# Where two gate-vector chunks of layer 0 are multiplied, and which memory the feed-forward weight buffers lie over

## The chip, the cores and the metric

The kernel runs on one core of a Trainium2 chip. The metric is the device time of one execution in microseconds (us). In the profile the engines are PE (TensorE), ACT (ScalarE), DVE (VectorE), POOL (GpSimd) and SP (SyncE, which here issues most of the DMA transfers); PEld is PE's loading of stationary operands.

## The reference, cut to what matters

Two layers work on 256 context tokens and 256 latent tokens of width 1024. The parts around the change:

```
mod = silu(c) @ mod_w[layer] + mod_b[layer]      # 6 vectors of 1024, for c and for c_ctx
sh1, sc1, g1, sh2, sc2, g2 = split(mod, 6)
x = x + g1 * even_mixer(rmsnorm(x, g) * (1 + sc1) + sh1)
x = x + g2 * conv_ffn(rmsnorm(x, g) * (1 + sc2) + sh2)
# layer 1: the same with odd_mixer, then a final rmsnorm
```

The mixer of layer 0 has two head groups (GLA and mLSTM), whose outputs are normalised, joined and multiplied by an output projection of 1024 x 1024. The feed-forward is an up projection to 2 x 2816 columns, a depthwise convolution, silu(g) * a, and a down projection.

## The kernel before, in words

Activations lie transposed, features on partitions and the 512 tokens along the free axis, so each 128 x 128 block of a weight is multiplied with 512 columns. For float32 accuracy each weight block and each activation is split into a high and a low half (wh, wl; hh, hl), and three matmuls (L186 to L188) make one product.

**Weights** come through `Stream` (L144): one load brings 16 blocks, 1 MB, into a raw tile; `split` turns 8 blocks, a unit, into wh by a copy on ACT (L174) and wl by a subtraction on DVE or POOL (L175), in the pool `wp` with 4 slots for each. `get` (L178) splits one unit ahead of the one in use. With a list `fill`, each load of a stream from number `skip` on also calls one function of the list (L161, L162), so that other work is spread over the stream.

**The modulation vectors** are such work. A chunk (layer, j) is 512 columns of `mod_w`: `mod_load` (L236) loads 2 MB in n pieces on SP, `mod_go` (L244) multiplies them on PE (L249) into a bank of PSUM given by `psa`, and `mod_out` (L266) copies the bank on ACT (L269), transposes it on PE in four pieces (L272) into a second bank of the same kind, and adds and scales on DVE (L276 to L280). Chunks 10 and 11 of a layer are g2, which only the feed-forward's residual (L339, component 5) reads. `mod_chunk` (L253) does load, multiply and output in one. The banks: `gps` 4, `mps` 3, `vps` 1.

**The order of layer 0.** `even_mixer` (L416) ends with four mLSTM heads (`head`, L670), the gates of that group (`gates`, L747, which also makes the first four pairs hh, hl), chunk 10, `finish` of heads 0 to 2 (L726: multiply, square, reduction, rsqrt, multiply, transposes L739, halves L740 and L741, each the k-th pair of the output projection for k = 4 to 7), chunk 11 and `finish(3)`. The raw tiles of chunks 10 and 11 are in `sp` under the tag b4, 4 slots, shared with the heads' tiles. Then comes the output projection with the stream WO, which uses the two raw slots of `rawp`: four column blocks at once over k (`gemm_k`), then four more one by one (`gemm_f`), each followed by its residual (L342) and a square for the norm. After it the norm's row is made (column sums L132, rsqrt on DVE L112 to L123, broadcast L140, copy L141), chunk (1,2) is multiplied with its raw tiles in `rawp`, and `norm_mod` (L314) makes the feed-forward's hh and hl.

**The feed-forward of layer 0** (`conv_ffn`, L828) goes in two halves of 11 steps. `project(j)` (L838) makes the g and a columns of step j, and calls for load j + 1 of the stream up0 in its second product; the banks are gps and mps, but mps and mps for the tenth step of a half and mps and vps for the eleventh, `project(10)`. The stream has the nine chunks of `fill1` (L387), from load 2 on. The convolution reads the bank with one ACT operation (L794) and ten DVE operations (L800). Before step 10's convolution the down projection starts (L864), whose stream dn0 shares the two raw slots of `rawp` with the chunks.

**Pools.** The order of the instructions on each engine and the waits are made by the Tile framework from the program order and the tiles' readers and writers. Pools opened after others have been closed lie over their memory. The mixer's pool `ep` starts with a2, lev, trineg, hblk, mk0, qk (two slots), mk1 and the cum tiles, later has mq, tok (two slots of 8.25 KB per partition, for gv and mv), sgg, RQT, wsT and ao, and ends there; `sp` follows. The feed-forward's pools start at the same address: before, `fp` (fcw and 22 half tiles, 45.7 KB per partition), `fs` (6 tiles y of 2 KB), then `ur` (two raw tiles of 8 KB for the up weights), which by these sizes lies over sgg, RQT, wsT, ao and the first b4 slot. In layer 1 `Conv` opens the same pools over those of `odd_mixer`; `last_ffn` puts chunk 10 of layer 1 and the down weights into its `ur`.

Of the kernel before, what the change touches and what calls it, by code (L numbers as in the profile page):

```python
# [9 lines left out]
F32 = mybir.dt.float32  # L10
# [6 lines left out]
P = 128  # L17
D = 1024
KD = 8
# [21 lines left out]
NFC = 44 * 10  # L41
# [10 lines left out]
def block_kernel(ctx: ExitStack, tc: tile.TileContext, A: dict, out: bass.AP):  # L52
    nc = tc.nc
    PSUM = bass.MemoryType.PSUM
    v, s, g, te = nc.vector, nc.scalar, nc.gpsimd, nc.tensor
# [8 lines left out]
    rawp = ctx.enter_context(tc.tile_pool(name="rawp", bufs=2))  # L64
# [32 lines left out]
    cv = load(A["cv"], [P, 16])  # L97
# [138 lines left out]
    def mod_load(l, j, pool=rawp, tag="raw", n=2, bufs=None):  # L236

        w = KD // n * 512
        for i in range(n):
            raw = pool.tile([P, w], F32, tag=tag, name=nm("rawm"), bufs=bufs)  # L240
            nc.sync.dma_start(out=raw, in_=A["modw"][l, j, :, i * w:(i + 1) * w])
            yield raw

    def mod_go(l, j, raws, psa):  # L244
        ps = psa()
        k = 0
        for raw in raws:
            for c in range(0, raw.shape[-1], 512):
                te.matmul(out=ps[32 * (k % 4):32 * (k % 4) + 32, :], lhsT=spad[:, k, :], rhs=raw[:, c:c + 512], start=k < 4, stop=k >= 4)  # L249
                k += 1  # L250
        mod_out(l, 4 * j, 4, ps, psa)

    def mod_chunk(l, j, pool=rawp, psa=vps, tag="raw", n=2, bufs=None):  # L253
        mod_go(l, j, mod_load(l, j, pool, tag, n, bufs), psa)

    def mod_part(q, pool, psa):

# [8 lines left out]
    def mod_out(l, c, n, ps, psa):  # L266

        ev = t2((P, n * P))
        s.copy(out=ev, in_=ps)  # L269
        pt = psa()[:, :n * P].rearrange("p (a b) -> p a b", b=P)  # L270
        for a in range(n):
            te.transpose(pt[:, a, :], ev[:, a * P:(a + 1) * P], ident)  # L272
        col = lambda name, o: pc(name, o, n).unsqueeze(2).to_broadcast([P, n, 2])
        i, k = c // KD, c % KD
        dst = comps[l][i][:, k:k + n, :]
        v.tensor_reduce(out=dst, in_=pt.rearrange("p a (q c) -> p a c q", q=4)[:, :, 0:2, :], axis=AX.X, op=ALU.add)  # L276
        v.tensor_tensor(out=dst, in0=dst, in1=col("modb", l * 48 + c), op=ALU.add)
        if i in (1, 4):

            v.scalar_tensor_tensor(out=dst, in0=dst, scalar=1.0, in1=col("nmg" if i == 1 else "nfg", l * 8 + k), op0=ALU.add, op1=ALU.mult)  # L280
# [33 lines left out]
    def norm_mod(l, comp_sh, comp_sc, segs, r, between=lambda k, acts: None, tiles=None):  # L314
        c0, c1 = segs[0][1], segs[-1][2]
        hs = [] if tiles is None else tiles
        sh, sc = comps[l][comp_sh], comps[l][comp_sc]
        acts = lambda k: hs[k]
        for k in range(KD):
            between(k, acts)  # L320
            y = t2()
            for ci, a, b in segs:
                v.scalar_tensor_tensor(out=y[:, a:b], in0=xT[k][:, a:b], scalar=sc[:, k, ci:ci + 1], in1=r[:, a - c0:b - c0],
                                       op0=ALU.mult, op1=ALU.mult)
            if tiles is None:
                hs.append(htiles(k))
            h_, l_ = hs[k]
            for ci, a, b in segs:
                s.activation(out=h_[:, a:b], in_=y[:, a:b], func=AF.Identity, bias=sh[:, k, ci:ci + 1])  # L329
            for ci, a, b in segs:  # L330
                v.scalar_tensor_tensor(out=l_[:, a:b], in0=y[:, a:b], scalar=sh[:, k, ci:ci + 1], in1=h_[:, a:b].bitcast(F32),  # L331
                                       op0=ALU.add, op1=ALU.subtract)
        return acts
# [18 lines left out]
    E = Ctx()  # L352
# [11 lines left out]
    with tc.tile_pool(name="stp", bufs=6) as stp:  # L364
        warm(10, ones)
        nrm = Norm(0, T)
# [9 lines left out]
        pss0 = [gps() for _ in range(4)]  # L376
# [7 lines left out]

        acts = norm_mod(0, 0, 1, SEGS, r, start)
    fill0 = [lambda j=j: mod_chunk(0, j) for j in (4, 5, 8, 9, 6, 7)]
    fill1 = [lambda j=j: mod_chunk(1, j) for j in (3, 0, 1, 4, 5, 8, 9, 6, 7)]  # L387
    E.fill0, E.W0 = fill0, W0
    nrm = Norm(0, T)
    with ExitStack() as st:  # L390
        even_mixer(E, st, acts, pss0, nrm.add)
    for k in range(KD):
        dump(f"x1_{k}", xT[k])
    r = nrm.row()
    mod_chunk(1, 2, rawp, mps)
    acts = norm_mod(0, 3, 4, SEGS, r)
    with ExitStack() as st:
        hs, nrms = [], [Norm(a, b) for _, a, b in SEGS]

        def then(m, sgs):  # L400
            for sg in sgs:
                nrms[sg[0]].add(m)
                if m == KD - 1:
                    hs[:] = hs or [htiles(k) for k in range(KD)]
                    norm_mod(1, 0, 1, (sg,), nrms[sg[0]].row(), tiles=hs)

        conv_ffn(E, st, acts, fill1, then)
# [8 lines left out]
def even_mixer(E, st, acts, pss0, then):  # L416
    nc, tc, A = E.nc, E.tc, E.A
    v, s, g, te = E.v, E.s, E.g, E.te
    pc, nm, mps, dump, ident, ones = E.pc, E.nm, E.mps, E.dump, E.ident, E.ones
# [3 lines left out]
    sp = st.enter_context(tc.tile_pool(name="sp", bufs=2))  # L423
# [34 lines left out]
    for j in range(2):  # L458
        lap = T_([P, 2, T], "b4", pool=sp, bufs=4)
        for d in range(2):  # L460
            ps = mps()
            te.matmul(out=ps, lhsT=a2[32 * d:32 * d + 32, j * P:(j + 1) * P], rhs=Gs[32 * d:32 * d + 32, :], start=True, stop=True)
            b = pc("gab", 2 * d + j)
# [296 lines left out]
    head(2)  # L760
    head(3)
    gates()
    E.mod_chunk(0, 10, sp, E.vps, "b4", 4, 4)
    finish(0)
    finish(1)
    finish(2)
    E.mod_chunk(0, 11, sp, E.vps, "b4", 4, 4)
    finish(3)
    for k in range(8):
        dump(f"m{k}", hh[k].bitcast(F32))  # L770
    WO = E.Stream(A["wout0"], 64)
# [4 lines left out]
    for m in range(4, KD):  # L776
        E.residual(0, 2, m, E.gemm_f(WO, 8 * m, KD, oa), SEGS)
        then(m)


class Conv:


    def __init__(self, E, st, l, n):
        self.E, self.n, self.lo = E, n, n - TL
        self.fp = st.enter_context(E.tc.tile_pool(name="fp", bufs=1))
        self.fs = st.enter_context(E.tc.tile_pool(name="fs", bufs=6))
        self.fcw = self.fp.tile([P, NFC], F32, tag="fcw", name=E.nm("fcw"))
        E.nc.scalar.dma_start(out=self.fcw, in_=E.A["fcw"][l])

    def centre(self, ps, ti):
        y = self.fs.tile([P, self.n], F32, tag="y", name=self.E.nm("y"))
# [35 lines left out]
def conv_ffn(E, st, acts, fill, then):  # L828

    v, g = E.v, E.g  # L830
    cv = Conv(E, st, 0, T)
    ur = st.enter_context(E.tc.tile_pool(name="ur", bufs=2))
    up = E.Stream(E.A["up0"], 44 * KD, fill, 1, 2, pool=ur, eng=lambda u: g)
    first = []
    per = FF // 2
    dn = E.Stream(E.A["dn0"], FF * KD, eng=lambda u: g if u * 8 % (per * KD) < per * 4 else v)

    def project(j):  # L838
        if j == 0:
            first.extend(E.gemm_k(up, 0, KD, acts, [(0, T)] * 4, [b() for b in (E.gps, E.mps, E.gps, E.mps)]))  # L840
        if 2 * j < len(first):
            pg, pa = first[2 * j:2 * j + 2]
        else:

            bg, ba = {per - 2: (E.mps, E.mps), per - 1: (E.mps, E.vps)}.get(j % per, (E.gps, E.mps))
            pg = E.gemm_f(up, 16 * j, KD, acts, 0, T, bg)
            pa = E.gemm_f(up, 16 * j + 8, KD, acts, 0, T, ba)
        return cv.centre(pg, FF + j), cv.centre(pa, j)

    for hf in range(2):  # L850
        hm = []
        b0 = hf * per * KD
        oa = lambda k: hm[k]
        pss, done = None, 0
        part = lambda: None
        nxt = project(hf * per)
        for jj in range(per):
            cg, ca = nxt
            if jj < per - 1:
                nxt = project(hf * per + jj + 1)  # L860

            if jj == per - 2:
                done = jj - 1
                pss = E.gemm_k(dn, b0, per, oa, [(0, T)] * 4, pss, range(done))  # L864
            h, part = cv.tile(cg, ca, g, part, jj)
            hm.append(h)
        part()
        last = hf == 1
        for m, ps in enumerate(E.gemm_k(dn, b0, per, oa, [(0, T)] * 4, pss, range(done, per))):
            E.residual(0, 5, m, ps, SEGS)  # L870
            if last:
                then(m, SEGS)
        for m in range(4, KD - 2 if last else KD):
            E.residual(0, 5, m, E.gemm_f(dn, b0 + m * per, per, oa), SEGS)
            if last:
                then(m, SEGS)

    for sg in SEGS:
        for m in (KD - 2, KD - 1):
            E.residual(0, 5, m, E.gemm_f(dn, b0 + m * per, per, oa, sg[1], sg[2]), (sg,), sg[1])  # L880
            then(m, (sg,))


def last_ffn(E, st, gated, out):
# [3 lines left out]
    v, s, g, te = E.v, E.s, E.g, E.te  # L888
    nm, mps = E.nm, E.mps
    cv = Conv(E, st, 1, TL)  # L890
    ur, dw, mw = (st.enter_context(tc.tile_pool(name=n, bufs=2)) for n in ("ur", "dw", "mw"))
    lp = st.enter_context(tc.tile_pool(name="lp", bufs=1))

    LAG = 4
# [25 lines left out]
    odd_out(E, gated, nrm.add, lambda: mods.extend((list(E.mod_load(1, 10, ur)), list(E.mod_load(1, 11, mw)))))  # L920
    turn(0)
    turn(4)
    E.mod_go(1, 10, mods[0], mps)
    r = nrm.row()
    E.mod_go(1, 11, mods[1], mps)
    acts = E.norm_mod(1, 3, 4, SEGS[1:], r)
    acc = [E.gps() for _ in range(4)]

# [465 lines left out]
```

## Time and profile before

| what | value |
|---|---|
| median of 3 runs | 1278.04 us (1277.53 to 1280.91) |
| the profiled execution | 1280.36 us |
| its span, first to last instruction | 1278.6 us |
| busy share of the span: PE, PEld, DVE, ACT, POOL | 96%, 78%, 73%, 46%, 33% |
| mean granted TensorE clock, as a share of full speed | 0.989 |

The profile shows one execution. The busy share is a mean over all stages; in a row of the timeline "x8" are eight instructions of one kind in a row, and the bracket is the idle time of the engine before them and what ended it.

### The profile page before, as it was taken

What the parts mean: (1) busy time and instruction counts of PE and PEld (TensorE: products, weight loads), DVE (VectorE), ACT (ScalarE), POOL (GpSimd) and SP (SyncE); (2) the same over time, 40 slices, a digit from 0 to 9 for tenths busy, and PEclk for the clock granted to TensorE, in tenths of its full rate; (3) what the DMA queues carried; (4) which work ended last, traced back from release to release, by engine and by line L of the source; (5) the groups of instructions that cost most, each with busy time, mean ns of one, the idle gap of its engine ahead of it and who ended that gap; (6) DMA issues with size and microseconds to landing.
All of it is one profiled execution on the core that took longest, in us unless ns stands there. A gap on an engine that the chain in (4) does not pass through costs nothing. (4 is left out here: it accounts for less than half of the span.)

```text
span 1278.6 us, 18743 instructions
## 1 busy us (share of the span) xinstructions
PE 1227.3 (96%) x7094; PEld 1001.2 (78%) x7094; DVE 928.4 (73%) x2064; ACT 593.9 (46%) x937; POOL 424.4 (33%) x246
## 2 busy tenths in 40 slices
PE   7989999999999999999999999999999998999996
PEld 5557787876867767888888897888887886999994
DVE  5483889487567776227776478888888955999997
ACT  4463345344344443214443246665656554655552
POOL 0100000000125555326666000022222314899992
PEclk9989999999999999999999999999999998999998
DMA  9556202334436565232211224453544394455431
GB/s 372 211 178 231 105 27 72 136 107 165 165 110 269 220 232 191 74 129 99 99 66 59 90 92 122 163 157 118 175 130 136 99 345 150 165 197 175 178 114 64
DMA packets 40107, 191.45 MB, mean 150 GB/s; under 512 B 4609, under 2 KB 10569, under 8 KB 21073
## 3 DMA queue, kind: packets, MB, share of 16 engines
q1 hardware_dynamic: 36512, 185.48, 41.6%
q10 hardware_dynamic: 3504, 4.77, 1.2%
q8 instruction: 56, 0.92, 0.3%
q14 instruction: 35, 0.28, 0.1%
HBM read 189.03 MB, written 1.20 MB: 149 GB/s over the span
## 5 line engine op out<-in xcount | busy, mean ns | idle before, releaser
L175 POOL TENSOR_TENSOR wl<-raw,wh 128x1024 fp32r<-128x1024 f32 x120 | 289.3, 2418 | 494.3 <-ACT wh L174 492.3
L174 ACT ACTIVATE wh<-raw 128x1024 fp32r<-128x1024 f32 x226 | 237.1, 1054 | 154.3 <-PE gps L188 98.2
L186 PE MATMUL gps<-hh,wh 128*128 128x512 f32 (+1 forms) x824 | 291.1, 354 | 6.9 <-ACT hh L329 4.9
L187 PE MATMUL gps<-hh,wl 128*128 128x512 f32 (+1 forms) x824 | 290.0, 352 | 1.1 <-DVE wl L175 1.1
L188 PE MATMUL gps<-hl,wh 128*128 128x512 f32 (+1 forms) x824 | 290.1, 353 | 0.0
L800 DVE SCALAR_TENSOR_TENSOR y<-mps,fcw,y 128x255 f32<-128x255 f32 (+3 forms) x592 | 245.5, 432 | 47.0 <-ACT y L794 33.5
L186 PEld LDWEIGHTS gps<-hh,wh 128*128 128x128 f32 x824 | 155.7, 189 | 42.9 <-issue 12.5
L175 DVE TENSOR_TENSOR wl<-raw,wh 128x1024 fp32r<-128x1024 f32 x106 | 129.8, 1234 | 78.0 <-ACT wh L174 77.9
L188 PE MATMUL mps<-hl,wh 128*128 128x256 f32 (+1 forms) x544 | 174.8, 322 | 1.4 <-DVE hl L331 1.4
L186 PE MATMUL mps<-hh,wh 128*128 128x256 f32 (+1 forms) x544 | 175.6, 323 | 0.3 <-ACT hh L329 0.3
L187 PE MATMUL mps<-hh,wl 128*128 128x256 f32 (+1 forms) x544 | 175.0, 322 | 0.0
L187 PEld LDWEIGHTS gps<-hh,wl 128*128 128x128 f32 x824 | 156.1, 189 | 24.0 <-issue 3.2
L188 PEld LDWEIGHTS gps<-hl,wh 128*128 128x128 f32 x824 | 156.1, 190 | 20.9 <-issue 1.7
L186 PEld LDWEIGHTS mps<-hh,wh 128*128 128x128 f32 x544 | 103.7, 191 | 15.5 <-issue 7.0
L188 PEld LDWEIGHTS mps<-hl,wh 128*128 128x128 f32 x544 | 103.5, 190 | 9.1 <-DVE hl L331 1.6
L187 PEld LDWEIGHTS mps<-hh,wl 128*128 128x128 f32 x544 | 103.6, 190 | 7.8
L800 DVE SCALAR_TENSOR_TENSOR y<-gps,fcw,y 128x189 f32<-128x189 f32 (+3 forms) x180 | 77.5, 438 | 22.0 <-ACT y L794 18.2
L794 ACT ACTIVATE y<-mps,fcw 128x256 f32<-128x256 f32 (+1 forms) x68 | 41.1, 638 | 89.0 <-PE mps L188 89.0
L186 PE MATMUL gps<-mh,wh 128*128 128x512 f32 (+1 forms) x198 | 73.5, 371 | 0.0
L188 PE MATMUL gps<-ml,wh 128*128 128x512 f32 (+1 forms) x198 | 73.5, 371 | 0.0
L187 PE MATMUL gps<-mh,wl 128*128 128x512 f32 (+1 forms) x198 | 73.4, 371 | 0.0
L342 DVE SCALAR_TENSOR_TENSOR x<-gps,mod,x 128x256 f32<-128x256 f32 x56 | 24.2, 478 | 45.1 <-PE gps L188 45.1
(293 smaller groups left out, 1899.5 us busy)
## 6 DMA issues: line engine op xcount, KB each, us to landing
raw<-in_up SPq DMA_DIRECT2D x42, 1024.0 KB, 4.9
rawm<-in_modw SPq DMA_DIRECT2D x36, 1024.0 KB, 6.7
raw<-in_win SPq DMA_DIRECT2D x32, 1024.0 KB, 5.3
raw<-in_dn SPq DMA_DIRECT2D x20, 1024.0 KB, 5.6
raw<-in_wout SPq DMA_DIRECT2D x10, 1024.0 KB, 6.2
rawm<-in_mods SPq DMA_DIRECT2D x8, 1024.0 KB, 14.2
R<-crd SPq DMA_DIRECT2D x32, 256.0 KB, 4.2
rawm<-in_modw SPq DMA_DIRECT2D x8, 512.0 KB, 6.3
```

The source lines that it names most:

```text
L174: s.activation(out=hi[:, :n], in_=rw, func=AF.Copy)
L175: self.eng(u).tensor_tensor(out=lo[:, :n], in0=rw, in1=hi[:, :n].bitcast(F32), op=ALU.subtract)
L186: te.matmul(out=ps, lhsT=lhi, rhs=rhi, start=first, stop=False)
L187: te.matmul(out=ps, lhsT=llo, rhs=rhi, start=False, stop=False)
L188: te.matmul(out=ps, lhsT=lhi, rhs=rlo, start=False, stop=last)
L342: v.scalar_tensor_tensor(out=xT[m][:, a:b], in0=ps[:, a - base:b - base], scalar=gt[:, m, ci:ci + 1], in1=xT[m][:, a:b], op0=ALU.mult, op1 ...
L794: self.E.s.activation(out=y, in_=ps, func=AF.Identity, scale=self.fcw[:, c + 4:c + 5], bias=self.fcw[:, c + 9:c + 10])
L800: self.E.v.scalar_tensor_tensor(out=o, in0=i, scalar=self.fcw[:, ti * 10 + wi:ti * 10 + wi + 1], in1=o, op0=ALU.mult, op1=ALU.add)
```

## The change

Chunks 10 and 11 of layer 0 are loaded in the mixer as before, but chunk 10 into the four b4 slots and chunk 11, in two pieces, into the two tok slots; both are multiplied after the output projection, in banks gps. `mod_go` now returns the output step as a function; chunk 11's is called after the norm. Chunk (1,2) moves to the head of the list `fill1`, which then has ten entries. `Conv` opens a small pool `fw` for fcw and `ur` ahead of `fp` and `fs`; by the sizes `ur` of layer 0 then lies over trineg, hblk, mk0, qk, mk1 and a little of cum.

```diff
-        mod_out(l, 4 * j, 4, ps, psa)
+        return lambda: mod_out(l, 4 * j, 4, ps, psa)
...
-        mod_go(l, j, mod_load(l, j, pool, tag, n, bufs), psa)
+        mod_go(l, j, mod_load(l, j, pool, tag, n, bufs), psa)()
...
-    fill1 = [lambda j=j: mod_chunk(1, j) for j in (3, 0, 1, 4, 5, 8, 9, 6, 7)]
+    fill1 = [lambda j=j: mod_chunk(1, j) for j in (2, 3, 0, 1, 4, 5, 8, 9, 6, 7)]
...
-        even_mixer(E, st, acts, pss0, nrm.add)
+        rest = even_mixer(E, st, acts, pss0, nrm.add)
...
     r = nrm.row()
-    mod_chunk(1, 2, rawp, mps)
     acts = norm_mod(0, 3, 4, SEGS, r)
+    rest()
...
     gates()
-    E.mod_chunk(0, 10, sp, E.vps, "b4", 4, 4)
     finish(0)
     finish(1)
     finish(2)
-    E.mod_chunk(0, 11, sp, E.vps, "b4", 4, 4)
     finish(3)
+
+    mods = [list(E.mod_load(0, 10, sp, "b4", 4, 4)), []]
+    for i in range(2):
+        raw = T_([P, 4, 516], "tok", bufs=2).rearrange("p a b -> p (a b)")[:, :2048]
+        nc.sync.dma_start(out=raw, in_=A["modw"][0, 11, :, i * 2048:(i + 1) * 2048])
+        mods[1].append(raw)
...
         E.residual(0, 2, m, E.gemm_f(WO, 8 * m, KD, oa), SEGS)
         then(m)
+    E.mod_go(0, 10, mods[0], E.gps)()
+    return E.mod_go(0, 11, mods[1], E.gps)
...
+        fw, self.ur = st.enter_context(E.tc.tile_pool(name="fw", bufs=1)), st.enter_context(E.tc.tile_pool(name="ur", bufs=2))
+        self.fcw = fw.tile([P, NFC], F32, tag="fcw", name=E.nm("fcw"))
+        E.nc.scalar.dma_start(out=self.fcw, in_=E.A["fcw"][l])
         self.fp = st.enter_context(E.tc.tile_pool(name="fp", bufs=1))
         self.fs = st.enter_context(E.tc.tile_pool(name="fs", bufs=6))
-        self.fcw = self.fp.tile([P, NFC], F32, tag="fcw", name=E.nm("fcw"))
-        E.nc.scalar.dma_start(out=self.fcw, in_=E.A["fcw"][l])
...
-    ur = st.enter_context(E.tc.tile_pool(name="ur", bufs=2))
-    up = E.Stream(E.A["up0"], 44 * KD, fill, 1, 2, pool=ur, eng=lambda u: g)
+    up = E.Stream(E.A["up0"], 44 * KD, fill, 1, 2, pool=cv.ur, eng=lambda u: g)
...
-    ur, dw, mw = (st.enter_context(tc.tile_pool(name=n, bufs=2)) for n in ("ur", "dw", "mw"))
+    ur = cv.ur
+    dw, mw = (st.enter_context(tc.tile_pool(name=n, bufs=2)) for n in ("dw", "mw"))
```

In `last_ffn` the two calls of `mod_go` get a pair of brackets more, and so do the same steps as before.

## Rows read from the trace of the kernel before

**Rows 1.** The page, busy time of PE, its share and its instructions

```profile
PE 1227.3 (96%) x7094; PEld 1001.2 (78%) x7094; DVE 928.4 (73%) x2064; ACT 593.9 (46%) x937; POOL 424.4 (33%) x246
```

**Rows 2.** Stretches: length, busy time (instructions) by engine, PEclk, DMA share, GB/s

```profile
296.80:355.14 58.34, 55.66 (x269) 41.53 (x269) 38.34 (x97) 18.88 (x30) 7.26 (x3) 1.00 0.49 166
355.14:363.97 8.83, 6.05 (x41) 3.22 (x40) 5.02 (x21) 3.71 (x7) 2.36 (x1) 1.00 0.46 166
364.20:367.60 3.40, 3.40 (x9) 2.65 (x9) 3.40 (x9) 1.88 (x5) 0.00 (x0) 0.50 1.01 426
...
476.38:489.84 13.46, 13.46 (x69) 9.74 (x68) 8.80 (x23) 5.08 (x7) 7.37 (x4) 1.00 0.63 236
...
1018.00:1063.60 45.60, 44.73 (x361) 41.42 (x359) 26.93 (x45) 20.68 (x29) 10.19 (x4) 1.00 0.90 330
```

**Rows 3.** Timeline of PE at the mixer's end: start, length, line, operation

```profile
296.80 1.07 PE L249 MATMUL vps<-rawm,spad 128*32 128x512 f32 x8
297.79 0.50 PE L186 MATMUL gps<-hh,wh 128*128 128x512 f32 x1
...
300.69 1.05 PE L249 MATMUL vps<-rawm,spad 128*32 128x512 f32 x4
304.43 1.05 PE L249 MATMUL vps<-rawm,spad 128*32 128x512 f32 x4 [2.69 <-DMA rawm<-in_modw]
...
306.45 0.60 PE L272 MATMUL vps<-c,t 128*128 128x128 f32 x4
306.80 0.48 PE L186 MATMUL gps<-hh,wh 128*128 128x512 f32 x1
```

**Rows 4.** Timeline of ACT, chunk 10's copy

```profile
305.53 0.59 ACT L269 COPY t<-vps 128x512 f32<-128x512 f32 x1 [3.76 <-PE vps L249]
```

**Rows 5.** Timeline of DVE: first reduction, last low half, first residual

```profile
306.68 0.69 DVE L733 TENSOR_REDUCE ssm<-t 128x4 f32<-128x512 f32 x1 [3.81 <-ACT t L731]
...
323.16 0.75 DVE L741 SCALAR_TENSOR_TENSOR hl<-mps,c,hh 128x512 fp32r<-128x512 f32 x1 [1.47 <-ACT hh L740]
...
331.54 0.88 DVE L342 SCALAR_TENSOR_TENSOR x<-gps,mod,x 128x256 f32<-128x256 f32 x2 [1.08 <-PE gps L188]
```

**Rows 6.** Timeline of PE in the norm before the feed-forward

```profile
358.19 1.92 PE L249 MATMUL mps<-rawm,spad 128*32 128x512 f32 x14
...
361.24 0.60 PE L140 MATMUL vps<-c,ry 128*128 128x128 f32 x4
...
363.97 0.60 PE L186 MATMUL gps<-hh,wh 128*128 128x512 f32 x1 [2.02 <-ACT hh L329]
```

**Rows 7.** Waits of SP, 300 to 340 us: total, times, longest

```profile
SPq L159 <- DVE qk L735: 14.7, 1, 14.7
```

**Rows 8.** DMA issues at 235 us: count, size, median time to landing

```profile
raw<-in_wout SPq DMA_DIRECT2D x2, 512.0 KB, 4.5
```

**Rows 9.** Timeline of PE in the feed-forward: ninth chunk, first vps products

```profile
489.84 1.92 PE L249 MATMUL vps<-rawm,spad 128*32 128x512 f32 x16
...
503.21 0.39 PE L186 MATMUL vps<-hh,wh 128*128 128x512 f32 x1
503.44 0.39 PE L187 MATMUL vps<-hh,wl 128*128 128x512 f32 x1
```

**Rows 10.** The page, groups: busy, mean ns of one, idle before and releaser

```profile
L175 POOL TENSOR_TENSOR wl<-raw,wh 128x1024 fp32r<-128x1024 f32 x120 | 289.3, 2418 | 494.3 <-ACT wh L174 492.3
L174 ACT ACTIVATE wh<-raw 128x1024 fp32r<-128x1024 f32 x226 | 237.1, 1054 | 154.3 <-PE gps L188 98.2
```

**Rows 11.** Timeline of SP in the second feed-forward half, no chunks there

```profile
580.41 65.60 SPq L159 DMA_DIRECT2D raw<-in_up  x7
```

**Rows 12.** Timeline of DVE: last reader of the ninth chunk's bank, vps convolution

```profile
493.61 0.19 DVE L276 TENSOR_REDUCE mod<-vps 128x8 f32<-128x32 f32 x1
...
509.74 4.61 DVE L800 SCALAR_TENSOR_TENSOR y<-vps,fcw,y 128x255 f32<-128x255 f32 x10 [0.83 <-ACT y L794]
```

**Rows 13.** Timeline of SP, first load of the down weights

```profile
490.97 0.33 SPq L159 DMA_DIRECT2D raw<-in_dn  x1
```

More of the change, by code (lines that the diff above doesn't have):

```diff
@@ L922, in last_ffn @@
     turn(4)
-    E.mod_go(1, 10, mods[0], mps)
+    E.mod_go(1, 10, mods[0], mps)()
     r = nrm.row()
-    E.mod_go(1, 11, mods[1], mps)
+    E.mod_go(1, 11, mods[1], mps)()
     acts = E.norm_mod(1, 3, 4, SEGS[1:], r)
```

## The prediction

> **What bounds the kernel now.** I read the engine shares first [rows 1]: TensorE (PE) is busy for 96% of the span, so a change pays where it takes away PE idle time, PE time at the low clock, or PE work. Next come the stages around the change [rows 2]. [...] The timelines of PE, ACT, DVE and SP then say what each gap waits for.
>
> **Chunks 10 and 11 leave the mixer's end.** PE executes in order, and the two chunks stand inside its projection work [rows 3]. A piece of chunk 10 delays the next matmul by 0.99 (296.80 to 297.79); the next takes 300.69 to 304.43 because the one after it sits 2.69 us on a load, and that one costs 0.98 more. Chunk 11 is three such pieces of 0.98, and each chunk has one group of transposes that costs 0.35 (306.45 to 306.80). Sum: 0.99 + 3.74 + 0.98 + 3 x 0.98 + 2 x 0.35 = 9.35 us. What is late next is the chain of finish: ACT idles 3.76 us before chunk 10's copy [rows 4], and DVE 3.81 before the first reduction, at 306.68, behind that copy [rows 5]. Without the chunks the chain starts up to 3.8 earlier, so the last low half, ready at 323.16 + 0.75 = 323.91, comes at 320.1. PE wants it for the last of eight k steps: the k loop ends near 331.5 [rows 5], a step is 12 matmuls 0.23 apart (503.21 to 503.44 [rows 9]), 2.8 us, so that step starts at 328.7 now and 319.4 then. Between a chain that stays (323.9 against 328.7: 4.8 saved) and the whole 9.35, I take **-9.0**, since the chain waited on the very copy that goes. Their loads stay ahead of the projection's last weight load on SP as before, 4 MB in six transfers instead of eight; the projection hides them, as the matmuls come 50 us later, and uncovered they would cost what the 2.69 did.
>
> **They enter the norm gap; chunk (1,2) leaves it.** Today's last vector matmul there ends 4.97 us after the projection (358.19 + 1.92 = 360.11), and the first feed-forward matmul comes 8.83 after it, at 363.97 [rows 6]. Chunk 10 takes chunk (1,2)'s place; chunk 11 adds 1.92 and chunk 10's transposes 0.35, so chunk 11 ends at 4.97 + 2.27 = 7.2. The rsqrt broadcast (at 361.24, 6.1 after) queues behind it, 1.1 late: by itself 1.1 us.
>
> Larger is what the weights do. The first feed-forward load stands on SP 14.7 us for qk, the multiply in the last finish [rows 7]. By the tile sizes in the code the weight buffers do not overlap qk now; they overlap sgg, ao and b4. So they wait for the whole old pool, not for the bytes below. After the change chunk 11's raw data are tok tiles of that pool, read until 7.2 after the projection. The first load then leaves at 7.2; half a megabyte lands 4.5 us later [rows 8], ACT splits it in 1.05 and POOL subtracts in 2.42 [rows 10]: 15.2 at the longest; with the first of the two halves a little ahead of the 4.5 median, 14.8. Against 8.83 that is **+6.0**, and the 1.1 is inside it. Bounds: +1.1 if the buffers wait only for the tiles below, +9 if the four POOL splits, now in the projection, slow DVE's norm. SP has nothing needed sooner behind the waiting load. The rest of chunk 11 (copy, transposes, three DVE steps) falls into the hole before the weights; uncovered, it would cost about the copy and the transposes, 0.59 [rows 4] and 0.35.
>
> The clock: the low stretch now spans 3.4 us [rows 2], 1.7 us of full-speed work. I keep it at **0**: more vector work in the gap could save the 1.7, the emptier wait from 7.2 to 14.8 could double it. [...]
>
> **Chunk (1,2) becomes a tenth filler.** A period with a filler chunk is 13.46 us [rows 2]; without one the seven issues from 580.41 (65.60 long, 0.33 the last issue) are 10.88 apart [rows 11]: 2.58 each. All later chunks move one load later, so the tenth falls in project(10), whose second half uses the single vps bank, as the chunk does. The ninth holds that bank from 489.84 to 493.80 (last reader, 493.61 + 0.19), 3.96 us [rows 9, 12], while other matmuls run on other banks. The tenth has nothing beside it: the vps matmuls (503.21) follow it and need the bank, so its cost is 3.96. Its raw tiles also take the two slots that the first down weights use (issued at 490.97 now [rows 13]); these go out after the tenth's first half, near 504.3, and are split by 504.3 + 4.5 + 1.05 + 2.42 = 512.3, when PE wants them at 508.6 + 3.96 = 512.6. I add 0.4 for a queue on ACT or POOL: **+4.4**. Bounds 2.58 and, if the bank goes to the projection first, the 14 of the second rival.
>
> **Layer 1.** The weight buffers move within the same old pool, so what they wait for stays. PE is busy 44.73 of 45.60 us at this boundary [rows 2]: at most 0.9 to gain, and no new wait. The small fcw load has no reader for 20 us. **0**.
>
> **Sum:** -9.0 + 6.0 + 4.4 = +1.4. The profiled execution took 1280.36 us (span 1278.6 plus 1.8 around it), so 1281.8; it lies 2.3 above the median of 1278.04, so 1279.4.
>
> **Rivals.**
> 1. *The feed-forward weights wait only for dead tiles.* For it: the new place of the buffers, over trineg, hblk, mk0, qk and mk1, is free 40 us earlier than the tok tiles. Against: the wait for qk [rows 7], whose bytes the load did not touch. The gap costs 1.1 in place of 6.0: -9.0 + 1.1 + 4.4 = -3.5, 1274.5; with a tenth chunk at 2.58, 1272.7.
> 2. *Slower: the vps bank goes to project(10) first.* Then the tenth chunk waits for the ten DVE steps that read it, until 509.74 + 4.61 = 514.35 [rows 12], and the down weights wait for the chunk. First half read at 515.3, weights split at 523.3, against 508.6: +14.7, sum +11.7, 1289.7, with 1.7 of low clock 1291.4. It decides as soon as the bank's owner is project(10) when the chunk's data have landed. Against it: the chunk's matmuls come first in program order.
> 3. *The change does not free PE.* The chain of finish stays as late as now, and only 4.8 is saved: -4.8 + 6.0 + 4.4 = +5.6, 1283.6. For it: DVE is the busiest engine of the chain; against it: the 3.8 us wait was for a copy that goes.
>
> **How the numbers follow.** About 0.3% (3.8 us) is what a measurement can tell here: faster is below 1274.2, slower above 1281.9. Forecast 0.45, own range 1276 to 1284 (its terms at -9.4 or -7, +4 or +8, +2.6 or +5, not all at once); rival 1 0.25, rival 2 0.15, rival 3 0.12; 0.03 for the rest. Faster: half of rival 1 and a tenth of the forecast, with the low end of the rest, 0.2; slower: rivals 2 and 3 with a fifth of the forecast, 0.36; the remaining 0.44 is no change. The range runs from rival 1's low end, 1272, to 1290, and leaves out about half of rival 2 and some tail.
>
> **What would show it.** The projection should end near 346 with no L249 between 296 and 340; the first feed-forward load should leave SP just after the last L249 of the gap, and the first matmul with hh and wl come some 14 to 15 us after the projection's last; ten L249 groups in the first feed-forward half, the last at the vps matmuls, with about 4 us before these go on. The forecast is wrong if that load leaves before the projection ends, if the tenth group comes after the vps matmuls, or if the projection shows gaps before its eighth k step.

## The result, and the profile after

The changed kernel took 1290.13 us (median; 1288.58 to 1295.02), the kernel before 1278.15 beside it: ratio 1.0092, 95% interval 1.0066 to 1.0117. That is 12.0 us slower. The prediction said no change, 1279.4, in a range from 1272 to 1290. That the result lies at the upper end of that range and not far outside is luck: the 1290 was set for the second rival, which did not happen.

I cut both profiled executions at the same events, by their starts: the first and the last of the copies that make hh from sgg (L752), the last tanh of the gates (L749), the projection's end (first column sum, L132), the first feed-forward matmul, the first centre copy of the convolution, the feed-forward's first residual, the first column sum of the next norm.

| stretch | before, us | after, us | difference | predicted |
|---|---|---|---|---|
| first to last copy from sgg | 13.94 | 17.35 | +3.4 | 0 |
| last tanh to the projection's end | 60.59 | 50.16 | -10.4 | -9.0 |
| projection's end to first feed-forward matmul | 8.83 | 14.18 | +5.4 | |
| that matmul to the first centre copy | 24.20 | 33.06 | +8.9 | |
| the last two together | 33.03 | 47.24 | +14.2 | +6.0 |
| first centre copy to first residual (first half) | 149.49 | 154.22 | +4.7 | +4.4 |
| second half, up to the sums of the next norm | 206.66 | 206.66 | 0 | 0 |

The sum is +11.9, and the medians differ by 12.0. The spans of the two profiles differ by 8.2 only (1286.8 against 1278.6), as the one of before has two stretches at half clock, at 84.32 and 1067.36 us, that the one after has not.

The stretches of the changed kernel, columns as in [rows 2]; the fourth and fifth lie inside the third:

```profile
296.42:346.58 50.16, 50.13 (x245) 41.80 (x246) 32.50 (x99) 16.54 (x29) 0.00 (x0) 1.00 0.30 106
346.58:360.76 14.18, 9.97 (x73) 4.03 (x71) 6.86 (x25) 4.21 (x8) 0.00 (x0) 1.00 0.32 114
360.76:393.82 33.06, 26.69 (x96) 20.89 (x97) 16.15 (x28) 12.57 (x22) 21.16 (x7) 0.79 0.45 170
361.10:367.90 6.80, 5.27 (x13) 3.69 (x12) 6.76 (x7) 2.94 (x7) 4.61 (x2) 0.50 0.74 273
374.76:381.56 6.80, 5.78 (x16) 4.61 (x17) 1.47 (x3) 0.00 (x0) 3.47 (x2) 0.50 0.33 107
393.82:548.04 154.22, 152.44 (x745) 112.47 (x744) 97.86 (x243) 58.59 (x78) 80.90 (x44) 1.00 0.53 200
```

Read the first row against the first of [rows 2]: the mixer's end has no PE idle time left (50.13 of 50.16), and POOL has nothing there, where before three weight splits lay (7.26). They are in the third row now: POOL is busy for 21.16 us, PE idles 6.37, and for 13.6 us the granted clock is 0.50, where before one stretch of 3.4 was.

The timeline of PE after the projection, to be read against [rows 6]:

```profile
349.62 1.92 PE L249 MATMUL gps<-rawm,spad 128*32 128x512 f32 x14
...
352.88 1.92 PE L249 MATMUL gps<-tok,spad 128*32 128x512 f32 x16
...
354.73 0.65 PE L140 MATMUL vps<-c,ry 128*128 128x128 f32 x4
...
356.06 1.92 PE L249 MATMUL vps<-rawm,spad 128*32 128x512 f32 x16 [0.68 <-ACT rstd L141]
...
360.76 0.96 PE L186 MATMUL mps<-hh,wh 128*128 128x512 f32 x2 [2.78 <-ACT wh L174]
...
363.25 0.80 PE L187 MATMUL mps<-hh,wl 128*128 128x512 f32 x1 [1.53 <-POOL wl L175]
...
375.78 0.79 PE L187 MATMUL mps<-hh,wl 128*128 128x512 f32 x1 [4.84 <-POOL wl L175]
```

Chunks 10 and 11 and then the first filler, chunk (1,2), are multiplied; then each wait is for a weight split: 2.78 for wh, 1.53 and 4.84 for wl. In [rows 6] the only wait of over 1 us was for hh (2.02). Why they are late is to be seen on SP (the changed kernel's timeline, DMA issues):

```profile
245.09 0.33 SPq L771 DMA_DIRECT2D tok<-in_modw  x1
...
354.86 0.33 SPq L159 DMA_DIRECT2D raw<-in_up  x1
```

on POOL, in the same kernel,

```profile
360.84 2.36 POOL L175 TENSOR_TENSOR wl<-raw,wh 128x1024 fp32r<-128x1024 f32 x1 [310.36 <-DMA raw<-in_up]
...
369.16 6.56 POOL L175 TENSOR_TENSOR wl<-raw,wh 128x1024 fp32r<-128x1024 f32 x1 [3.45 <-ACT wh L174]
```

and on DVE:

```profile
252.77 0.35 DVE L700 SCALAR_TENSOR_TENSOR b<-b,RQT,c_trineg 128x128 f32<-128x128 f32 x1 [3.03 <-DMA b<-prd]
...
361.14 2.34 DVE L331 SCALAR_TENSOR_TENSOR hl<-t,mod,hh 128x256 fp32r<-128x256 f32 x1 [1.45 <-ACT hh L329]
363.40 2.60 DVE L323 SCALAR_TENSOR_TENSOR t<-x,mod,rstd 128x256 f32<-128x256 f32 x1
```

The first feed-forward load leaves SP at 354.86, right behind chunk 11's last L249 and 8.3 us after the projection; before it left at 322.54. The splits therefore run beside DVE's norm. A split that took 2.42 on the mean of the kernel before [rows 10] takes 6.56 there, and DVE operations of 0.47 take 2.34 and 2.60. The first row of SP and the first of DVE belong to another effect, 100 us earlier, which comes at the end of the part on the prediction.

### The profile page after: what moved, and what is told of

Its sections match the earlier page's. It is cut to its first block, busy times and chain, and to the rows that moved or that the text cites. A ratio compares the mean times of both kernels' runs of the same rounds, so it can differ in the third digit from the quotient of the medians.

```text
span 1286.8 us, 18739 instructions
## 1 busy us (share of the span) xinstructions
PE 1225.5 (95%) x7094; PEld 1003.0 (78%) x7094; DVE 926.7 (72%) x2064; ACT 593.5 (46%) x937; POOL 428.4 (33%) x246
## 5 line engine op out<-in xcount | busy, mean ns | idle before, releaser
L175 POOL TENSOR_TENSOR wl<-raw,wh 128x1024 fp32r<-128x1024 f32 x120 | 294.1, 2458 | 488.1 <-DMA raw<-in_up 310.4
```

Of the source, the lines that this page charges most:

```text
L175: self.eng(u).tensor_tensor(out=lo[:, :n], in0=rw, in1=hi[:, :n].bitcast(F32), op=ALU.subtract)
```

## The experiments

Theory A: the late weights make the gap. Theory B: the multiplies of the three chunks make it. Theory C: the tenth filler is what costs. Ratios are to the kernel before on the same chip.

**1. Weights that wait only for the bytes they take.**

```diff
-        fw, self.ur = st.enter_context(E.tc.tile_pool(name="fw", bufs=1)), st.enter_context(E.tc.tile_pool(name="ur", bufs=2))
+        kw = {} if l else {"reuse_waits": "tile"}
+        fw, self.ur = (st.enter_context(E.tc.tile_pool(name=n, bufs=b, **kw)) for n, b in (("fw", 1), ("ur", 2)))
```

> The changed kernel, but in layer 0 the weight buffers wait only for the tiles whose bytes they take, not for the whole old pool. Theory A (late weights: the first feed-forward load leaves only after chunk 11, so the splits fall into the norm and PE waits for them): the load leaves SP before 330 us, PE has no wait for wh or wl after the projection, the first centre copy comes 33 to 35 us after the projection's end instead of 47.2, and the time falls by 12 to 14, to 1276 to 1278. Theory B (the multiplies of chunks 10, 11 and (1,2), not the weights, fill the gap): only the two waits of 2.78 and 1.53 us before the third matmul go, 1286. Theory C (the tenth filler is what costs): no change in the time beyond 2 us.

Measured: 1289.44 us, ratio 1.0092 (1.0070 to 1.0115); projection's end to first centre copy 46.48. No gain, though the loads were early, as SP's timeline of this kernel shows:

```profile
330.00 0.38 SPq L159 DMA_DIRECT2D raw<-in_up  x1
...
330.95 0.66 SPq L159 DMA_DIRECT2D raw<-in_up  x1
```

ACT's timeline has the squares of the projection, the norm's copies and the first split:

```profile
348.62 0.63 ACT L294 ACTIVATE t<-x 128x512 f32<-128x512 f32 x1 [4.81 <-DVE x L342]
...
357.43 1.31 ACT L329 ACTIVATE hh<-t,mod 128x256 fp32r<-128x256 f32 x3 [0.55 <-DVE t L323]
358.64 1.04 ACT L174 ACTIVATE wh<-raw 128x1024 fp32r<-128x1024 f32 x1
```

POOL's has that split's subtraction,

```profile
359.76 11.32 POOL L175 TENSOR_TENSOR wl<-raw,wh 128x1024 fp32r<-128x1024 f32 x1 [308.31 <-ACT wh L174]
```

and PE's the matmul that waits for it:

```profile
371.14 0.80 PE L187 MATMUL mps<-hh,wl 128*128 128x512 f32 x1 [10.67 <-POOL wl L175]
```

The last of the three loads landed at 340.2. ACT idles 4.81 us before 348.62 with data ready, yet its first split comes at 358.64, behind three hh copies of the norm: in the changed kernel, too, the first split stands behind three hh copies (356.56, then 359.65). ACT took its operations in their order here, though the data of the split lay ready, and the splits' place in that order had not moved with the loads. POOL then took 11.32 us for the first one, and PE waited 10.67. So A as I put it falls: early data are not enough. The time by itself is what theory C gave; PE's wait of 10.67 speaks against C, and experiments 2 and 5 decide on it. A2: what matters is where the splits stand in the order, inside the norm or in the projection ahead of it.

**2. Chunk 11 in the raw slots of `rawp`.** Now nothing in the old pool `ep` is read after the last finish, so the wait of the weights ends early and the framework can order the splits early.

```diff
-    mods = [list(E.mod_load(0, 10, sp, "b4", 4, 4)), []]
-    for i in range(2):
...
+    mods = [list(E.mod_load(0, 10, sp, "b4", 4, 4))]
...
-    return E.mod_go(0, 11, mods[1], E.gps)
+    return E.mod_go(0, 11, E.mod_load(0, 11), E.gps)
```

> The changed kernel, but chunk 11's raw data lie in the two raw slots that chunk (1,2) had, not in the old pool's tok tiles; the waits by pool stay. Theory A: the last reader of the old pool under the weight buffers is again the multiply of the last finish, so the load leaves near 314 us, and the gap closes as with the other experiment: 1276 to 1278; chunk (1,2) is then loaded after chunk 11 and multiplied later. Theory B: 1286 to 1288. Theory C: 1288 to 1292.

Measured: 1276.44 us, ratio 0.9993 (0.9975 to 1.0011). The first splits on its POOL:

```profile
329.32 2.41 POOL L175 TENSOR_TENSOR wl<-raw,wh 128x1024 fp32r<-128x1024 f32 x1 [277.12 <-ACT wh L174]
334.71 2.43 POOL L175 TENSOR_TENSOR wl<-raw,wh 128x1024 fp32r<-128x1024 f32 x1 [2.98 <-ACT wh L174]
```

Its stretches from the projection's end to the first feed-forward matmul and from there to the first centre copy, columns as in [rows 2]:

```profile
344.20:355.14 10.94, 8.05 (x57) 3.61 (x55) 4.94 (x20) 3.71 (x7) 2.36 (x1) 1.00 0.49 166
355.14:381.31 26.17, 26.17 (x112) 17.98 (x113) 12.07 (x34) 11.08 (x19) 7.21 (x3) 0.93 0.37 134
```

The splits are in the projection again at 2.4 each, PE has no idle time after the first matmul, and from the projection's end to the first centre copy it takes 37.11: 10.1 of the 14.2 us are back. The load left at 313.18. That decides for A2 and against B and C: the same multiplies stand in the same gap. The 2.1 before the first matmul that stay (10.94 against 8.83) are PE order: the broadcast L140 starts 8.16 after the projection, 6.10 before. The other 2.0 lie behind the first matmul and were not broken down. The time fell by 13.7, more than these 10.1, because the first stretch of the table is back as well, 13.81 here.

**3. The pools alone, and the chunks alone.** The kernel before with the new order of the pools; and the changed kernel with the old order.

```diff
+        fw, self.ur = ...
+        self.fcw = fw.tile([P, NFC], F32, tag="fcw", name=E.nm("fcw"))
...
-        self.fcw = self.fp.tile([P, NFC], F32, tag="fcw", name=E.nm("fcw"))
```

(The second kernel has this edit the other way round.)

> The kernel before with the new order of the feed-forward pools alone; chunks 10, 11 and (1,2) stay where they were. Theory A: the weight buffers wait for the whole old pool wherever they lie in it, so the first load leaves SP where it did, at 322.5 us after the multiply of the last finish, and the time is that of before, 1277 to 1280. The rival, that buffers wait only for the tiles below them: the load leaves before 300 us, with the same time, since nothing waits for these weights in the kernel before.

> The changed kernel with the feed-forward pools in the order of before, so the weight buffers lie over sgg, RQT, wsT, ao and the first b4 slot. If the buffers wait for whole old pools and the splits are ordered by that, the place inside them is without effect: the load leaves after chunk 11's last matmul, and the time is that of the changed kernel, 1287 to 1292. Rival: the new place makes the change better or worse than the move of the chunks alone, by over 5 us either way.

Measured: pools alone 1278.26 us, ratio 0.9996 (0.9977 to 1.0015), first load at 322.42; chunks alone 1287.47, ratio 1.0083 (1.0062 to 1.0105), first load at 355.06, projection's end to first centre copy 47.07. Both as expected: inside one old pool the place of the buffers is without effect, and, as far as these times can tell, the whole loss comes with the chunks.

**4. POOL beside DVE, measured by itself.** The kernel before with four POOL subtractions of 512 columns that nothing reads, once from the norm's row, once from its third hl.

```diff
+    junk = np_.tile([P, 512], F32, tag="junk", name="junk", bufs=1)
+    for _ in range(4):
+        g.tensor_tensor(out=junk, in0=r, in1=r, op=ALU.subtract)
     acts = norm_mod(0, 3, 4, SEGS, r)
```

(The second one has the loop after this line, with in0=acts(2)[1].)

> The kernel before with four additional POOL subtractions of 512 columns on a tile of their own, started by the norm's row, so that they run beside DVE's norm; nothing reads them. By the weight splits' 2.41 us for 1024 columns each would take 1.2 alone. Theory (POOL gets no turn while DVE works without a break): the first takes more than 4 us, until DVE's first idle time, and single DVE operations take 2 us and more in place of 0.47. Rival (both share evenly, or don't meet): each takes 1.2 to 2.4, and DVE's operations stay under 1 us.

> The kernel before with the four additional POOL subtractions started by the third hl of the norm, when DVE is already at work without a break, in place of the norm's row, where POOL began together with DVE and took 1.15 us for each. Nothing reads them. Theory (the engine that is at work keeps the other out; POOL gets no turn until DVE idles): the first takes 4 us or more, up to DVE's first idle time, the others about 1.2, and one DVE operation behind them over 1 us. Rival (POOL's turns come between DVE's operations in any case): each takes 1.2 to 1.7 as before.

POOL's timeline in the first, where POOL and DVE begin together,

```profile
360.17 4.58 POOL L398 TENSOR_TENSOR junk<-rstd 128x512 f32<-128x512 f32 x4 [3.65 <-ACT rstd L141]
```

and DVE's beside it:

```profile
360.13 3.72 DVE L323 SCALAR_TENSOR_TENSOR t<-x,mod,rstd 128x256 f32<-128x256 f32 x3
```

In the second DVE was at work already when POOL began:

```profile
369.48 4.65 POOL L399 TENSOR_TENSOR junk<-hl,rstd 128x512 f32<-128x512 f32 x1 [8.91 <-DVE hl L331]
...
374.20 2.75 POOL L399 TENSOR_TENSOR junk<-hl,rstd 128x512 f32<-128x512 f32 x2
```

DVE's timeline there has the pause and what follows:

```profile
374.56 4.12 DVE L331 SCALAR_TENSOR_TENSOR hl<-t,mod,hh 128x256 fp32r<-128x256 f32 x3 [1.60 <-ACT hh L329]
378.61 2.63 DVE L323 SCALAR_TENSOR_TENSOR t<-x,mod,rstd 128x256 f32<-128x256 f32 x1
```

Both kernels ran once, so only their traces are used. The first expectation missed: POOL was not held up at all (1.15 each), and DVE paid, 3.72 for three operations that took 1.27 in the kernel before. The second came out as expected: POOL's first operation took 4.65, until DVE's pause of 1.60; the others 1.3 to 1.4. So each kept the other out. POOL, once it had its turn, let single DVE operations through between its own (three in 3.72); DVE, working on end, let POOL in only late: here at its pause of 1.60, in experiment 1 and in the changed kernel at the last hl of the norm, which then took 2.57 (at 368.80) and 2.56 (at 373.45). That the 11.32 and the 6.56 of the splits are the same effect is read from these traces, and not shown by a run of its own.

**5. The tenth filler.** Chunk (1,2) back ahead of the norm with nine fillers; and the tenth with load 12.

```diff
-    fill1 = [lambda j=j: mod_chunk(1, j) for j in (2, 3, 0, 1, 4, 5, 8, 9, 6, 7)]
+    fill1 = [lambda j=j: mod_chunk(1, j) for j in (3, 0, 1, 4, 5, 8, 9, 6, 7)]
...
+    mod_chunk(1, 2, rawp, mps)
     acts = norm_mod(0, 3, 4, SEGS, r)
```

```diff
+    fill1.insert(9, lambda: None)
```

> The changed kernel, but chunk (1,2) is again multiplied ahead of the norm, and the list has nine fillers. In the changed kernel's trace the first feed-forward half loses 4.0 us between the centre copies 6 and 21. Theory A: just these 4 come back, the gap stays as long as it is (first centre copy 47 us after the projection's end), 1286. Theory B: the gap gets longer by the 1.9 us of the chunk's matmuls or stays, 1286 to 1288. Theory C: 8 to 12 come back, 1278 to 1282.

> The changed kernel, but the tenth filler goes with load 12 instead of 11, into the second feed-forward half, past the vps matmuls of project(10). In the changed kernel the first half loses 4.7 us between the centre copies 0 and 21. If this loss is the tenth chunk at the vps bank and the down weights behind it, it falls to under 1 there, the second half pays 2 to 2.6, and the time falls by 2 to 3, to 1287 to 1288; the gap at the norm stays as it is. Rival: the loss is that all ten chunks stand one load later, and stays at 4 or more: 1290 to 1292.

Measured: nine fillers 1287.70 us, ratio 1.0082 (1.0051 to 1.0113); load 12: 1286.75, ratio 1.0069 (1.0042 to 1.0095). With nine fillers the first centre copy to the first residual takes 149.48, all 4.7 back, and the gap 46.39, 0.85 less; the medians give only 2.4, but the two intervals overlap widely. With load 12 the stretches (after the gap: first half, second half) are

```profile
395.39:545.67 150.28, 149.64 (x725) 111.72 (x724) 97.24 (x241) 57.77 (x77) 80.94 (x44) 1.00 0.51 192
545.67:754.90 209.23, 209.23 (x954) 171.24 (x952) 123.37 (x272) 70.42 (x95) 92.99 (x49) 1.00 0.28 96
```

so 3.9 come back in the first half and 2.6 are paid in the second, net 1.4; the medians say 3.4, again with intervals that overlap. C falls, by the stretches: of the 11.9 us the tenth filler has 4.7, the gap 14.2.

**6. The parts put together.** Experiment 2 with the tenth filler at load 12; the same with chunk 11 multiplied after the norm's row; and this last with the old order of the pools.

```diff
     r = nrm.row()
+    mod_chunk(0, 11, rawp, mps)
     acts = norm_mod(0, 3, 4, SEGS, r)
```

> Chunk 11 in the raw slots of rawp, as in the earlier experiment (1276.4), and the tenth filler with load 12. If the two effects add: 1273 to 1275. Rival: with the feed-forward on time, a filler in the second half costs as much as in the first: 1276 to 1277.

> Chunk 10 after the projection from the b4 slots, chunk 11 after the norm's row from the raw slots, so that the rsqrt broadcast no longer stands behind chunk 11 on PE, and the tenth filler with load 12. If the broadcast sets the end of the gap, it saves 1 to 2 us against the same without that move: 1271.5 to 1274, faster than before by 0.3 to 0.5%. Rival: the gap ends with the norm's vectors whatever stands ahead of the broadcast: 1273 to 1275.

> The fastest version so far (chunk 10 after the projection, chunk 11 after the norm's row from the raw slots, tenth filler with load 12; 1271.0) with the feed-forward pools in the order of before. Its weight buffers then reach into the second old pool, whose b4 tiles chunk 10 reads after the projection. By the theory the splits fall into the norm again and 10 to 15 us are lost: 1281 to 1286. Rival: the wait for chunk 10 alone, 4 us after the projection, is short enough to be hidden, 1271 to 1275.

Measured: the first 1276.00 us, ratio 0.9980 (0.9964 to 0.9997), its rival's number, with 10.94 and 26.47 from the projection's end to the first matmul and on to the first centre copy; the second **1271.00**, ratio 0.9944 (0.9925 to 0.9963), faster than both kernels; the third 1277.07, ratio 0.9994 (0.9978 to 1.0009). The same two stretches of the second and of the third:

```profile
346.16:356.37 10.21, 8.57 (x61) 4.06 (x60) 4.84 (x21) 4.19 (x8) 2.36 (x1) 1.00 0.44 136
356.37:379.08 22.71, 22.71 (x108) 17.28 (x109) 14.15 (x34) 10.27 (x19) 11.41 (x3) 1.00 0.42 156
```

```profile
342.89:354.44 11.55, 8.57 (x61) 4.06 (x59) 5.94 (x25) 4.58 (x9) 0.00 (x0) 1.00 0.46 168
354.44:380.78 26.34, 25.73 (x108) 19.19 (x109) 23.25 (x30) 12.43 (x20) 17.68 (x7) 0.87 0.50 183
```

In the fastest version the broadcast L140 starts 6.21 after the projection, as before, and chunk 11 fills the time in which PE waited for hh; the granted clock stays at 1.00, and the two rows give 32.92, less than the 33.03 of before with one chunk more in them. Against the first kernel's 37.41 that is 4.5 less, but only 0.7 of it lies ahead of the first matmul, where the broadcast was to save time. The other 3.8 lie behind it: there the first kernel has a stretch of 3.4 us at half clock and chunk (1,2) in three pieces, this one neither. As the edit also gives chunk 11 another bank and its output at once, what the order alone is worth is not shown.

POOL's timeline of this fastest version has a long split too:

```profile
363.41 9.04 POOL L175 TENSOR_TENSOR wl<-raw,wh 128x1024 fp32r<-128x1024 f32 x2 [13.49 <-ACT wh L174]
```

The first of these two took 6.48, until DVE's last hl of the norm. PE had no idle time all the same (22.71 of 22.71), since the four units that it needed first had been split ahead of the norm. So a split that was held cost nothing by itself here; it cost where PE needed that unit next, 4.84 in the changed kernel and 10.67 in experiment 1.

With the pools in the old order the weight buffers reach into `sp`, where chunk 10 is; the load leaves at 347.95, the first units are split inside the norm (POOL: 17.68 against 11.41), and it is 37.89. Here no split took more than 2.7; DVE was kept out instead, with four operations of the norm of 2.6 each in place of 0.47. The loss of 6.1 us by the medians, 5.0 by these rows, lies between the two expectations: the load was released 5.1 after the projection, not 8.3. So the new order of the pools is worth these 5 to 6 us, but only where chunk 11 is kept out of `ep`; in the change as it was made it is worth nothing.

## Why the prediction was right or wrong

**Chunks leave the mixer's end: right, undersized.** -10.4 against -9.0, 1.1 beyond my bound of -9.35. Counted from the projection's first matmul, which stood behind a piece of 0.99 [rows 3], 9.15 went (57.35 to 48.19), 0.8 more than my pieces gave without that one. The trace of the kernel before shows where such a rest comes from: the matmul behind a piece takes 0.34 to the next, the one behind the transposes 0.32, and the one ahead of two of the pieces 0.33, where 0.23 is usual [rows 9]; my 0.98 and 0.35 left these tenths out. And the 2.69 us on a load are those of one execution: 1.03, 2.34 and 2.35 in the three other traces with the chunks in that place (experiments 3 and 4), whose stretch took 58.97 to 61.82 in place of 60.59. The chain of finish did move with the copy that went; rival 3 (1283.6) was wrong.

**The norm gap: the step that failed.** The release of the weights was named right, the size of the term wrong: "They wait for the whole old pool" holds (354.86, behind the last L249), but the term measured +14.2, not +6.0, and its upper bound of +9 was too low. My sum went as far as the first unit: 7.2 + 4.5 + 1.05 + 2.42 = 15.2, taken as 14.8. The first matmul with hh and wl came 16.7 after the projection (363.25), 1.9 later. What I left out is what came behind it. The later units have no term in the sum, so they stood at nothing without a reason, and of POOL and DVE together I weighed only that DVE's norm might be slower. In fact the third split was held for 6.56, PE waited 4.84 for it, and in each of the two groups of waits the clock fell: 361.10 to 367.90 and 374.76 to 381.56 at 0.50. Experiment 1 has the extreme, 11.32 and 10.67. The long split is only one form of it: with nine fillers (experiment 5) no split took more than 2.7, four DVE operations took 2.3 to 2.6 instead, and the gap was still 46.39. Smaller, and inside the 14.2: the broadcast came 8.15 after the projection (354.73), 2.05 later than before and not 1.1, as PE waited 0.75 for the copy of chunk 10 ahead of its transposes, a wait that my 0.35 did not have.

Why DVE and POOL kept each other out there was not shown. Experiment 4 shows it in both orders, and that POOL did not come in after one DVE operation of 0.48: its first took 4.65, up to DVE's pause.

**Rival 1 (weights wait only for dead tiles): false, and its price too.** The trace denies the mechanism; experiment 1 made it true and still gave 1289.4, not 1274.5, because the splits' place in the order did not follow the loads.

**The clock.** I put 0, an estimate between a gain of 1.7 and a loss of 1.7. No run shows that term, nor that more multiplies alone save it: two stretches of 6.8 us at half clock stand where one of 3.4 was. PE was busy for 5.27 + 5.78 us in them, so some 5.5 us of full-speed work lost against 1.7 before: by this estimate +3.8 us of the 14.2. In the fastest version no wait of PE in the gap was over 0.75 us, and the clock stayed at 1.00. The extra multiplies by themselves did not keep it up, neither in the changed kernel (0.79 from the first feed-forward matmul to the first centre copy) nor in the last one of experiment 6 (0.87 in its second row).

**The tenth filler: right.** +4.7 against +4.4. From its matmuls (509.74) to the vps matmuls (513.46) it took 3.72 (I said 3.96); 0.8 stay when it is moved away. It came ahead of the vps matmuls, so rival 2 was false: its number, 1289.7, is near the result for another reason.

**Layer 1: right**, 0 within what the two profiles can tell.

**A term that I did not have, +3.4.** I wrote that the chunks' loads "stay ahead of the projection's last weight load on SP as before". One half of chunk 11 does not: the first of the two tok slots is free after the GLA heads, and its load of 1 MB leaves at 245.09, right ahead of the small loads b and t that the mLSTM heads wait for. DVE waited 3.03 us for b, 1.22 for t before; PE idled 2.48 instead of 0.65, and a stretch of 3.4 us at half clock followed at 255.28. In the kernel before the longest such wait of DVE in the same place is this one (DVE's timeline):

```profile
252.73 0.69 DVE L691 TENSOR_TENSOR t<-t,mq 128x512 f32<-128x512 f32 x1 [1.22 <-DMA t<-prd]
```

In the five kernels with chunk 11 in tok DVE waits 2.7 to 3.1 us for b, and the copies from sgg take 15.5 to 17.4 us (the lower two without that stretch at half clock); in the eight without they take 13.1 to 13.9. That comparison rests on the traces; no run moved this load alone.

With the gap at +14.2 and this term my sum would have been 1278 - 9.0 + 14.2 + 4.4 + 3.4 = 1291.

## What to carry to other kernels

Before buffers are laid over dead tiles, look for the last reader of the whole pool under them: one tile that is read late holds back everything that lands on that pool, and by the order of the program also the work that feeds on it. Price a late transfer by what its consumers then meet, not by its own chain: here the splits met the norm on a pair of engines that kept each other out (a split of 2.42 took 6.56, DVE operations of 0.47 took 2.34 and 2.60), and around the waits the granted clock was 0.50 for 13.6 us. When a step is moved to a hole, try it behind what the hole is waiting for (chunk 11 after the broadcast, with its bank and output changed too: 1276.0 to 1271.0 us), and see when its loads will leave.

## What the runs showed of the hardware that was not expected

- A POOL subtraction of 2.4 us took 11.32 in experiment 1, while DVE worked on end on the norm (L323, L331); one of 1.15 took 4.65, up to DVE's pause. Whether it cost time depended on who needed the result: PE waited 10.67 for that of the 11.32, and 6.48 in the fastest version cost it nothing. The other way round, POOL's four took 1.15 each and three DVE operations 3.72 in place of 1.27.
- Beside the convolution's DVE operations in the feed-forward of layer 0 the splits kept their 2.4 us: in the changed kernel 38 of them lie beside these operations, with a mean of 2.41 and none over 2.42. Why these and not the norm's was not shown.
- With a 1 MB load issued at 245.09, less than 1 us ahead of small loads on another queue (245.55 to 246.41), DVE waited 3.03 us for one of those, against 1.22 at most in the kernel before, without it. This is read from traces; no run has this load as its only difference.
